# Output projection and first feed-forward product of a hybrid decoder layer: other banks, weight sums one tile ahead, token sums in another buffer, and column groups interleaved

## The chip, the cores and the metric

The kernel runs on one core of one Trainium2 chip. The metric is device time in microseconds (us) of the whole program. The engines are called PE (matrix products and transposes), DVE (vector), ACT (scalar functions and copies), POOL (GpSimd) and SP, which here only starts transfers between the chip's memory and the core's on-chip memory. Each engine takes its own instructions in order; an instruction whose input or output is not ready holds everything behind it on that engine.

## The reference

One decoder layer over 2048 tokens of width 1024, in float32:

```
nx = rmsnorm(x);  proj = nx @ w_in
o_a = gated linear attention heads;  o_b = dilated sliding-window attention heads
h = x + concat(o_a, o_b) @ w_out
nm = rmsnorm(h)
a = square(relu(nm @ w_ff1))        # 1024 -> 4096
h = h + a @ w_ff2                   # 4096 -> 1024
out = rmsnorm(h)
```

The change touches the third line (the output projection), the norm behind it, and the product with `w_ff1`, called FF1 below.

## The kernel before

Each float32 operand is split into a high part that the matrix engine takes and a low remainder: `split` (L483 to L485) writes the high part on ACT (L484) and the remainder on DVE (L485). `mm3` (L138 to L142) forms one product by three matmuls, high by high (L140), low by high (L141) and high by low (L142). A 128x512 split is thus one ACT and one DVE instruction.

Blocks of a matrix product are multiplied by a scheme of 7 products in place of 8: sums and differences of the four blocks of each operand are formed first, and the 7 products are added into accumulators that the blocks of the result share. The products are numbered 1 to 7 and are taken in the order 1, 2, 6, 5, 7, 3, 4.

The program runs in stages: the input projection (to about 520 us), attention and linear attention (to about 870), the output projection (to about 1067), FF1 for the first 1024 tokens (to about 1385) and for the second 1024 (to about 1690), then the second feed-forward product. The Python code writes the work in a certain order; a scheduler then places the instructions of each engine, so that the order on an engine is not always the order of the code. Accumulators lie in eight banks with tags: two "a", three "c", two "d", one "o". `ps("a")` takes the next bank with tag "a", and waits until its last reader is done.

The output projection starts with four rows of 128 tokens, the loop `for at in range(4)` from L1520, each as a plain product with 96 matmuls. `plain_rows` (L1512) transposes the mixed heads of a row with PE and splits them into `mT`, in two halves q = 0, 1 (banks "c" and "d"). Each row uses two accumulators with tag "a", to which a copy of `x` is added on DVE (L1541, tile `xh`). Beside it, `mix_wo` (from L1111) loads two chunks of `w_out` into `wtraw`, forms four differences on POOL (L1118), and splits them into `wb`; it is called once for each of the four rows, in that row. The first rows overlap with the end of the attention, whose branches are combined by L927 to L950 on DVE and POOL (tiles `gla`, `small`, `O`, `cmb`). The rest of the projection goes by 7 products: `product0(g)` for g from 14 to 55, of 12 matmuls each, with `prep0` forming the operand (`mcomb`) from raw copies that ACT makes of the transposed heads (`raw_block`, tile `ar`, L1467).

After each row `norm_row` (L1257) normalizes it, transposes it with PE (L1266), and lets ACT copy it into `bb` (L1267), which is stored to `hTD`. After each pair of rows `norm_sums` (L1270) forms four sums of the blocks on DVE in place in `bb` (L1274 to L1277) and stores them to `hTD` too. So FF1 later reads each of the 7 operand sums of the tokens from `hTD`: `token_pieces` (L1282) loads 14 pieces, two for each product, into `rb` (L1290), and splits each into `hb`, at a pace of 5 pieces in 4 jobs, counted from the argument `first`.

FF1 is a list of jobs: 32 groups of columns (16 for each token half) by 7 products, 12 matmuls a job. `prep1(at + 2)` forms the weights of the job two ahead: it splits a block of `w1raw` into one of four buffers `w1comb`, and at products 2 and 6 updates `w1raw` (L1366 to L1370). At products 7 and 4 it starts the load of the weights two groups on (L1351), one half of the group each; there are two such buffers, for even and odd groups. `product1` multiplies; accumulators come from `bank()`, which walks through the tags "a c d c a d c o", and their results leave by ACT (L1434) or DVE (L1436, L1440, L1444), then a relu and a square on ACT (L1425, L1426, L1449). Sums of the results for the next product are formed by `act_sums` (L1398), three steps a job.

Of the kernel before, what the change touches and what calls it, by code (L numbers as in the profile page):

```python
# [66 lines left out]
SUMS = [line.split() for line in SUMS.splitlines()]  # L67
EARLY = 5
SINGLE = {0: "a10", 1: "a13", 2: "a32", 22: "a01"}
# [45 lines left out]
def emit(tc, a, stop=99):  # L115
# [1135 lines left out]
    def store_T(t, *which):  # L1251
        half, i = t // HT, t % 4
        for j, q in which:
            SP.dma_start(hTD[half, j - 1][:, :, i * 128:i * 128 + 128], hb4[q])

# [13 lines left out]

    def norm_sums(t):  # L1270

        b11, b21, b12, b22 = hb4
        V.tensor_tensor(b12, b12, b11, op=OP.subtract)
        V.tensor_tensor(b22, b22, b12, op=OP.subtract)  # L1274
        V.tensor_tensor(b21, b21, b22, op=OP.subtract)
        V.tensor_tensor(b11, b22, b11, op=OP.subtract)
        store_T(t, (5, 2), (6, 3), (4, 1), (7, 0))  # L1277

    turns = [0]

    def token_pieces(half, first):

        parts_at = {}
        for n in range(14):
            parts_at.setdefault(first + 1 + n * 4 // 5, []).append(n)
        piece = lambda n: rb[n // 2 % 2][:, 1024 * (n % 2):1024 * (n % 2) + 1024]
# [5 lines left out]
        def step(at):  # L1292
            if at == first - 3:
                while len(rb) < 2:
                    rb.append(slot("rb"))
                for n in range(4):
                    load(n)
            for n in parts_at.get(at, ()):
                j = order[n // 2]
                if j not in TF:  # L1300
                    TF[j] = [slot(f"hb{j}", FR) for _ in range(2)]
                    TB[j] = [view(v, (4, 512)) for v in TF[j]]
                cs = slice(1024 * (n % 2), 1024 * (n % 2) + 1024)
                split(*[v[:, cs] for v in TF[j]], piece(n))
                load(n + 4)
# [35 lines left out]
    order = (1, 2, 6, 5, 7, 3, 4)  # L1341
    jobs1 = [(g, j) for g in range(2 * NP) for j in order]
    raw1, combs1, acc1 = [], [], []
# [59 lines left out]
    def product1(at):  # L1403
# [12 lines left out]
        if j in (1, 2, 5):  # L1416
            banks[j] = bank()
        p = banks[{6: 1, 7: 1, 4: 1, 3: 5}.get(j, j)]
        B, W = TB[j], combs1[at % 4]
# [23 lines left out]
        elif j == 3:  # L1443
            V.tensor_tensor(c12, p, X, op=OP.add)  # L1444
            square(c12)
            single(1)
        else:
            A.activation(c21, p, AF.Relu)
            A.activation(c21, c21, AF.Square)  # L1449
            single(2)  # L1450
            sums1.append(act_sums(half, q, both, SUMS[EARLY:] if par else SUMS[:EARLY]))

# [33 lines left out]
    def row_done(p, e):  # L1486
# [3 lines left out]
        if e:  # L1490
            norms.append((norm_sums, t))

# [19 lines left out]
    def plain_rows(p, e):  # L1512
        m = view(slot("mT", FR), (2, CH, 128))
        for q in range(2):
            split(*[m[:, i, 4 * q:4 * q + 4] for i in range(2)], mix_block(p, e, q, "cd"[q]))
        return m

    load_mix(0)
    nxt = plain_rows(0, 0)
    for at in range(4):  # L1520
        p, e = divmod(at, 2)
# [8 lines left out]
        if at == 1:  # L1530
            nxt = plain_rows(1, 0)
        mix_wo(at)
        b = [ps("a"), ps("a")]
        parts_ = 2 if at < 2 else 1
# [9 lines left out]
        if at == 3:  # L1544
            for q, e in ((0, 0), (1, 0), (0, 1), (1, 1)):
                raw_block(2, e, q)
            load_mix(3)
            for g in range(14, 17):
                prep0(g)
    half0, half1 = token_pieces(0, -7), token_pieces(1, 7 * (NP - 1))  # L1550
    for g in range(14, 56):
# [163 lines left out]
    for at in range(len(jobs1)):  # L1715
        prep1(at + 2)
        some_sums()
        product1(at)
# [100 lines left out]
```

## Time and profile before

| quantity | value |
|---|---|
| median of 3 runs | 2274.73 us (2273.97 to 2284.05) |
| profiled execution | 2281.68 us |
| its span, first to last instruction | 2279.8 us |
| PE busy | 2231.8 us (98%) |
| DVE busy | 1694.4 us (74%) |
| ACT busy | 1250.1 us (55%) |
| POOL busy | 502.2 us (22%) |
| mean granted clock of PE | 0.990 |

Times in the rows below are counted from the start of the span. In a timeline row the first number is the start, the second the length, then engine, line, operation, the tile written and the tiles read, the shape and a count; in brackets stands the idle time of the engine before it and what ended that idle time. A matmul row's length includes its tail in the array; matmuls that follow each other overlap, so their pace is read from the starts.

### The profile page before, as it was taken

What the parts mean: (1) busy time and instruction counts of PE and PEld (TensorE: products, weight loads), DVE (VectorE), ACT (ScalarE), POOL (GpSimd) and SP (SyncE); (2) the same over time, 40 slices, a digit from 0 to 9 for tenths busy, and PEclk for the clock granted to TensorE, in tenths of its full rate; (3) what the DMA queues carried; (4) which work ended last, traced back from release to release, by engine and by line L of the source; (5) the groups of instructions that cost most, each with busy time, mean ns of one, the idle gap of its engine ahead of it and who ended that gap; (6) DMA issues with size and microseconds to landing.
All of it is one profiled execution on the core that took longest, in us unless ns stands there. A gap on an engine that the chain in (4) does not pass through costs nothing.

```text
span 2279.8 us, 35292 instructions
## 1 busy us (share of the span) xinstructions
PE 2231.8 (98%) x12436; PEld 1928.3 (85%) x12436; DVE 1694.4 (74%) x3172; ACT 1250.1 (55%) x2483; POOL 502.2 (22%) x471
## 2 busy tenths in 40 slices
PE   9999999999999998899999999999999999999998
PEld 8978998799999997787788887888888888888876
DVE  8788877766777677767767678767786697566778
ACT  6665436425877873455555557555555433333435
POOL 1210002024385674200000000000006322032462
PEclk9999999999999999999999999999999999999999
DMA  6467754776757965677745456554479997767775
GB/s 206 129 186 243 250 156 133 221 239 221 225 194 237 285 204 196 216 228 249 225 128 164 128 164 210 157 176 146 144 250 278 315 303 266 220 236 254 255 260 177
DMA packets 363602, 482.80 MB, mean 212 GB/s; under 512 B 20197, under 2 KB 269558, under 8 KB 353184
## 3 DMA queue, kind: packets, MB, share of 16 engines
q1 hardware_dynamic: 358926, 471.89, 63.8%
q0 software_dynamic: 4352, 8.39, 2.0%
q8 instruction: 98, 1.61, 0.3%
q14 instruction: 80, 0.66, 0.1%
q10 hardware_dynamic: 146, 0.27, 0.0%
HBM read 330.74 MB, written 154.44 MB: 213 GB/s over the span
## 4 chain that ended last, share of the span: by engine, by line
PE 85%; DMA 5%; DVE 4%; issue 3%; ACT 2%; POOL 1%; SPq 0%; POOLq 0%; DVEq 0%; ACTq 0%
PE ps_a L141 8%; PE ps_a L140 8%; PE ps_a L142 8%; PE ps_c L141 8%; PE ps_c L142 8%; PE ps_c L140 8%; PE ps_a L890 4%; PE ps_d L141 4%; PE ps_d L140 4%; PE ps_d L142 4%; PE ps_o L142 4%; PE ps_o L141 4%; PE ps_o L140 4%; PE ps_d L871 3%; PE ps_c L853 2%
## 5 line engine op out<-in xcount | busy, mean ns | idle before, releaser
L1640 POOL TENSOR_TENSOR bs<-bs,rb 128x1024 f32<-128x1024 f32 x60 | 178.3, 2982 | 1036.9 <-DMA actD<-ring 792.5
L485 DVE TENSOR_TENSOR cb<-bs,cb 128x1024 fp32r<-128x1024 f32 x104 | 162.5, 1563 | 137.3 <-ACT cb L484 137.2
L484 ACT ACTIVATE cb<-bs 128x1024 fp32r<-128x1024 f32 x104 | 110.3, 1060 | 281.2 <-issue 141.0
L485 DVE TENSOR_TENSOR w1comb<-w1raw,w1comb 128x512 fp32r<-128x512 f32 x224 | 153.5, 687 | 87.7 <-ACT w1comb L484 87.7
L862 ACT ACTIVATE pe<-pe,O 128x256 f32<-128x256 f32 (+1 forms) x384 | 157.9, 453 | 53.8 <-DVE O L861 51.8
L890 PE MATMUL ps_a<-v,pt 128*128 128x65 f32 x1200 | 181.1, 255 | 5.4 <-ACT pt L878 5.4
L484 ACT ACTIVATE w1comb<-w1raw 128x512 fp32r<-128x512 f32 x224 | 139.5, 625 | 79.9 <-PE ps_c L142 28.9
L890 PEld LDWEIGHTS ps_a<-v,pt 128*128 128x128 f32 x1200 | 176.3, 196 | 7.2 <-ACT pt L878 6.0
L871 PE MATMUL ps_d<-ident,pe 128*128 128x128 f32 x600 | 160.8, 282 | 0.0
L861 DVE CUSTOM_DVE_ANT_0 pe<-ps_c,nb 128x256 f32<-128x256 f32 (+1 forms) x384 | 126.5, 360 | 44.2 <-PE ps_d L871 17.5
L284 ACT ACTIVATE wcomb<-wraw 128x512 fp32r<-128x512 f32 (+2 forms) x119 | 90.0, 757 | 99.3 <-PE ps_a L141 35.3
L140 PE MATMUL ps_c<-hb,w1comb 128*128 128x512 f32 x336 | 130.9, 390 | 0.0
L141 PE MATMUL ps_c<-hb,w1comb 128*128 128x512 f32 x336 | 130.7, 389 | 0.0
L142 PE MATMUL ps_c<-hb,w1comb 128*128 128x512 f32 x336 | 130.7, 389 | 0.0
L485 DVE TENSOR_TENSOR ca<-ra,ca 128x1024 fp32r<-128x1024 f32 x84 | 118.6, 1412 | 5.8 <-ACT ca L484 5.8
L141 PE MATMUL ps_c<-cb,ca 128*128 128x512 f32 x312 | 121.9, 391 | 0.0
L140 PE MATMUL ps_c<-cb,ca 128*128 128x512 f32 x312 | 121.9, 391 | 0.0
L142 PE MATMUL ps_c<-cb,ca 128*128 128x512 f32 x312 | 121.9, 391 | 0.0
L1425 ACT ACTIVATE acc<-acc 128x512 f32<-128x512 f32 x96 | 60.7, 632 | 93.6 <-DVE acc L1440 41.8
L871 PEld LDWEIGHTS ps_d<-ident,pe 128*128 128x128 f32 x600 | 110.4, 188 | 0.3
L349 POOL TENSOR_TENSOR acc<-acc,misc 128x264 f32<-128x264 f32 (+1 forms) x32 | 39.1, 1236 | 313.7 <-DVE acc L348 287.3
L142 PE MATMUL ps_a<-wcomb,tb 128*128 128x256 f32 (+1 forms) x344 | 97.7, 284 | 0.0
(457 smaller groups left out, 7195.8 us busy)
## 6 DMA issues: line engine op xcount, KB each, us to landing
ra<-actD SPq DMA_DIRECT2D x52, 1024.0 KB, 7.6
actD<-ring SPq DMA_DIRECT2D x176, 256.0 KB, 3.4
rb<-w_ff SPq DMA_DIRECT2D x88, 512.0 KB, 5.9
bs<-w_ff SPq DMA_DIRECT2D x72, 512.0 KB, 6.0
w1raw<-w_ff SPq DMA_DIRECT2D x64, 512.0 KB, 4.2
k<-kD SPq DMA_DIRECT2D x16, 1024.0 KB, 7.7
hTD<-bb SPq DMA_DIRECT2D x56, 256.0 KB, 3.9
rb<-hTD SPq DMA_DIRECT2D x28, 512.0 KB, 5.7
```

What stands on the lines that cost most here:

```text
L140: T.matmul(out, sh, mh, start=first, stop=False, **kw)
L141: T.matmul(out, sl, mh, start=False, stop=False, **kw)
L142: T.matmul(out, sh, ml, start=False, stop=last, **kw)
L284: A.activation(hi, src, AF.Copy, scale=sc)
L484: A.activation(hi, src, AF.Copy)
L485: V.tensor_tensor(lo, src, hi.bitcast(F32), op=OP.subtract)
L861: V.tensor_tensor_reduce(p, s, bias, scale=1.0, scalar=BIG, op0=OP.add, op1=OP.min, accum_out=nm)
L862: A.activation(p, p, AF.Exp, bias=nm, scale=-1.0)
L871: T.transpose(pb[:, i * 128:i * 128 + 128], src, ident)
L890: T.matmul(self.b.opsum[:, n % 4], self.pt[:, i * 128:i * 128 + 128], self.b.v[:, blk, cols], start=first, stop=last)
L1425: A.activation(v, v, AF.Relu)
L1640: (engines or ((G,), (V, V))[len(sums) - 1])[e].tensor_tensor(v, v, r, op=OP.add if op == "+" else OP.subtract)
```

## The change

It has five parts. (1) The transposes of the four plain rows all go through banks "c", and their accumulators alternate between "a" (even rows) and "d" (odd rows). (2) `mix_wo` is called one row earlier, for the first row ahead of the loop; in the last row the raw blocks, the load of the next mixed heads and the first two operands are formed ahead of that row's matmuls, not behind them. (3) `norm_sums` writes three of its four sums into the row's `xh` tile, which is no longer needed for the row itself, so they need not wait until the stores of `bb` have read it. (4) The pieces of the token operands come at a pace given by an argument: 110 hundredths of a job each in the first half, 130 in the second, with other starts. (5) In the first pair of groups, in the last of the first token half and in the first of the second half, the jobs of the two groups are interleaved, which also makes the banks belong to a group each, and the sums of the odd group come in two parts.

```diff
-EARLY = 5
+EARLY, LATE = 5, 12
...
-    def norm_sums(t):
+    def norm_sums(t, x):
         b11, b21, b12, b22 = hb4
+        t2, t4, t3 = [view(v, (4, 128)) for v in (x[:, 0, :512], x[:, 0, 512:], x[:, 1, :512])]
         V.tensor_tensor(b12, b12, b11, op=OP.subtract)
-        V.tensor_tensor(b22, b22, b12, op=OP.subtract)
-        V.tensor_tensor(b21, b21, b22, op=OP.subtract)
-        V.tensor_tensor(b11, b22, b11, op=OP.subtract)
-        store_T(t, (5, 2), (6, 3), (4, 1), (7, 0))
+        V.tensor_tensor(t2, b22, b12, op=OP.subtract)
+        V.tensor_tensor(t4, b21, t2, op=OP.subtract)
+        V.tensor_tensor(t3, t2, b11, op=OP.subtract)
+        store_T(t, (5, b12), (6, t2), (4, t4), (7, t3))
...
-    def token_pieces(half, first):
+    def token_pieces(half, first, pace):
         parts_at = {}
         for n in range(14):
-            parts_at.setdefault(first + 1 + n * 4 // 5, []).append(n)
+            parts_at.setdefault(first + n * pace // 100, []).append(n)
...
-            if at == first - 3:
+            if at == first - 4:
...
-    jobs1 = [(g, j) for g in range(2 * NP) for j in order]
+    apart = [(g, j) for g in range(2) for j in order]
+    mixed = [(0, 1), (0, 2), (0, 6), (1, 1), (0, 5), (1, 2), (0, 7), (1, 6), (0, 3), (1, 5), (0, 4), (1, 7), (1, 3), (1, 4)]
+    jobs1 = [(g + n, j) for g in range(0, 2 * NP, 2) for n, j in (mixed if g in (0, NP - 2, NP) else apart)]
...
-            banks[j] = bank()
-        p = banks[{6: 1, 7: 1, 4: 1, 3: 5}.get(j, j)]
+            banks[par, j] = bank()
+        p = banks[par, {6: 1, 7: 1, 4: 1, 3: 5}.get(j, j)]
...
+            if par:
+                sums1.append(act_sums(half, q, both, SUMS[EARLY:LATE]))
...
-            sums1.append(act_sums(half, q, both, SUMS[EARLY:] if par else SUMS[:EARLY]))
+            sums1.append(act_sums(half, q, both, SUMS[LATE:] if par else SUMS[:EARLY]))
...
     def plain_rows(p, e):
         m = view(slot("mT", FR), (2, CH, 128))
         for q in range(2):
-            split(*[m[:, i, 4 * q:4 * q + 4] for i in range(2)], mix_block(p, e, q, "cd"[q]))
+            split(*[m[:, i, 4 * q:4 * q + 4] for i in range(2)], mix_block(p, e, q, "c"))
...
     nxt = plain_rows(0, 0)
+    mix_wo(0)
     for at in range(4):
...
-        mix_wo(at)
-        b = [ps("a"), ps("a")]
+        if at < 3:
+            mix_wo(at + 1)
+        if at == 3:
+            for n in range(4):
+                raw_block(2, n % 2, n // 2)
+            load_mix(3)
+            for g in range(14, 16):
+                prep0(g)
+        b = [ps("ad"[e]), ps("ad"[e])]
...
         if at == 3:
-            for q, e in ((0, 0), (1, 0), (0, 1), (1, 1)):
-                raw_block(2, e, q)
-            load_mix(3)
-            for g in range(14, 17):
-                prep0(g)
-    half0, half1 = token_pieces(0, -7), token_pieces(1, 7 * (NP - 1))
+            prep0(16)
+    half0, half1 = token_pieces(0, -6, 110), token_pieces(1, 7 * (NP - 2) + 3, 130)
...
-        some_sums()
+        some_sums(4 if jobs1[at][0] // 2 in (NP // 2 - 1, NP // 2) and at % 14 < 5 else 3)
```

What the change moves in the finished program is seen best on the engines. First PE, at the end of row (0,0) of the projection and the start of row (0,1), before (a name such as `wo` or `wb` is a part of the weights, `mT` the transposed row):

```order
L140 MATMUL ps_a<-wo,mT 128x512
L141 MATMUL ps_a<-wo,mT 128x512
L142 MATMUL ps_a<-wo,mT 128x512
L140 MATMUL ps_a<-wb_9282,mT 128x512 [waits DVE_49]
L141 MATMUL ps_a<-wb_9282,mT 128x512
```

And at the same place after the change:

```order
L1337 MATMUL ps_c<-ident,O_9446 128x128 [waits DVE_49]
L141 MATMUL ps_a<-wo,mT 128x512
L142 MATMUL ps_a<-wo,mT 128x512
L140 MATMUL ps_a<-wo,mT 128x512
L141 MATMUL ps_a<-wo,mT 128x512
L142 MATMUL ps_a<-wo,mT 128x512
L141 MATMUL ps_d<-wb_9282,mT 128x512 [waits DVE_49]
L142 MATMUL ps_d<-wb_9282,mT 128x512
```

The new row writes to a bank "d" and waits for the row's own operand on DVE, no longer for the add that frees a bank "a"; one transpose of the attention's output (`O`) now stands inside the old row.

Second POOL, at the last combine of the attention (L927 to L950) and the first weight sums (L1118), before:

```order
L930 TENSOR_TENSOR gla<-gla,O_9446 128x8
L930 TENSOR_TENSOR gla<-gla,cmb 128x8 x2
L934 TENSOR_TENSOR gla<-gla,O_9446 128x8
L936 TENSOR_TENSOR gla<-gla,cmb 128x8
L937 TENSOR_TENSOR gla<-gla 128x8
L936 TENSOR_TENSOR gla<-gla,cmb 128x8
L937 TENSOR_TENSOR gla<-gla 128x8
L942 TENSOR_TENSOR gla<-gla 128x8 x3
```

And after:

```order
L1118 TENSOR_TENSOR wtraw<-wtraw 128x512
L930 TENSOR_TENSOR gla<-gla,O_9446 128x8
L930 TENSOR_TENSOR gla<-gla,cmb 128x8 x2
L1118 TENSOR_TENSOR wtraw<-wtraw 128x512
L934 TENSOR_TENSOR gla<-gla,O_9446 128x8
L936 TENSOR_TENSOR gla<-gla,cmb 128x8
L1118 TENSOR_TENSOR wtraw<-wtraw 128x512 x2
L937 TENSOR_TENSOR gla<-gla 128x8
L936 TENSOR_TENSOR gla<-gla,cmb 128x8
L937 TENSOR_TENSOR gla<-gla 128x8
L942 TENSOR_TENSOR gla<-gla 128x8 x3
```

The four sums of the first set stand between POOL's combine steps, where before the first of them came after the whole combine.

Third PE, at the end of the projection, where FF1's first jobs begin (`w1comb` their weights, `hb` the tokens, `xh` the last rows to be transposed), before:

```order
L140 MATMUL ps_d<-hb_11518,w1comb 128x512 [waits Activation_49]
L1266 MATMUL ps_c<-ident,xh 128x128 [waits DVE_49,PE_49]
L1266 MATMUL ps_c<-ident,xh 128x128 x3
L1266 MATMUL ps_c<-ident,xh 128x128 [waits PE_49]
L1266 MATMUL ps_c<-ident,xh 128x128 x3
L140 MATMUL ps_c<-hb_11451,w1comb 128x512 [waits PE_49]
L141 MATMUL ps_a<-hb_11428,w1comb 128x512 [waits DVE_49]
L142 MATMUL ps_a<-hb_11429,w1comb 128x512
```

And after:

```order
L1266 MATMUL ps_c<-ident,xh 128x128 [waits DVE_49,PE_49]
L1266 MATMUL ps_c<-ident,xh 128x128 x3
L1266 MATMUL ps_c<-ident,xh 128x128 [waits PE_49]
L1266 MATMUL ps_c<-ident,xh 128x128 x3
L140 MATMUL ps_c<-hb_11467,w1comb 128x512 [waits PE_49,Activation_49]
L140 MATMUL ps_d<-hb_11428,w1comb 128x512 [waits Activation_49]
L141 MATMUL ps_a<-hb_11428,w1comb 128x512 [waits DVE_49]
L142 MATMUL ps_a<-hb_11429,w1comb 128x512
```

In both, first matmuls of later jobs are moved ahead of the rest of the first job (bank "a"). The one into bank "d" is now that of the second group's first product, the fourth job, and it reads the first product's tokens.

More of the change, by code (lines that the diff above doesn't have):

```diff
@@ L1253, in store_T @@
         for j, q in which:
-            SP.dma_start(hTD[half, j - 1][:, :, i * 128:i * 128 + 128], hb4[q])
+            SP.dma_start(hTD[half, j - 1][:, :, i * 128:i * 128 + 128], hb4[q] if isinstance(q, int) else q)
     def norm_row(h, t):
```

2 lines of the change are left out of this document (1 added, 1 removed).

## The prediction

> **What bounds the kernel now.** I read the page's totals first, then the list of what the matrix engine (PE) waited for, then the granted clock in the stretches behind its long waits, and last the instructions of the engines it waited for.
>
> ```profile
> span 2279.8 us, 35292 instructions
> ...
> PE 2231.8 (98%) x12436; PEld 1928.3 (85%) x12436; DVE 1694.4 (74%) x3172; ACT 1250.1 (55%) x2483; POOL 502.2 (22%) x471
> ```
>
> PE is busy for 98% of the span, and the change leaves its matmuls as they are. So the change can win only what PE idles, and what it loses in clock, in the stretches that the diff touches: the first four rows of the output projection, the start of FF1, and the start of FF1's second token half. The waits of PE there are these (line, what it waited for, us in total, times, longest), the first row from 860 to 895 us, then two from 920 to 940, five from 1050 to 1100, four from 1376 to 1410:
>
> ```profile
> PE ps_a L140 <- DVE xh L1541: 4.0, 1, 4.0
> ...
> PE ps_c L1266 <- ACT ar L1467: 4.0, 1, 4.0
> PE ps_c L1336 <- ACT ar L1467: 2.2, 1, 2.2
> ...
> PE ps_a L140 <- ACT xs L1434: 5.4, 1, 5.4
> PE ps_d L141 <- DVE mcomb L485: 1.7, 1, 1.7
> PE ps_a L140 <- ACT w1comb L484: 1.5, 1, 1.5
> PE ps_d L140 <- ACT stats L173: 1.3, 1, 1.3
> PE ps_d L140 <- ACT acc L1434: 0.2, 1, 0.2
> ...
> PE ps_d L141 <- DVE w1comb L485: 1.7, 1, 1.7
> PE ps_o L140 <- ACT acc L1434: 0.9, 1, 0.9
> PE ps_d L140 <- ACT xs L1434: 0.5, 1, 0.5
> PE ps_d L140 <- ACT acc L1434: 0.5, 1, 0.5
> ```
>
> They sum to 4.0, 6.2, 10.1 and 3.6 us: 23.9 us. Behind the three longest the clock was low (stretch, its length, busy time of PE, PEld, DVE, ACT, POOL with counts, granted clock, DMA share, GB/s):
>
> ```profile
> 885.00:891.00 6.00, 5.96 (x15) 4.71 (x16) 5.99 (x10) 1.65 (x4) 0.00 (x0) 0.54 0.49 122
> 932.00:935.00 3.00, 3.00 (x9) 2.50 (x10) 2.50 (x4) 3.00 (x7) 0.00 (x0) 0.51 0.93 287
> 1091.00:1096.00 5.00, 4.79 (x12) 3.43 (x13) 1.77 (x3) 3.74 (x9) 0.00 (x0) 0.56 0.66 201
> ...
> 1060.00:1080.00 20.00, 17.17 (x79) 13.69 (x78) 18.07 (x24) 13.77 (x24) 0.00 (x0) 1.00 0.88 294
> 1080.00:1092.00 12.00, 6.44 (x30) 4.74 (x30) 11.99 (x15) 6.96 (x11) 0.00 (x0) 0.86 0.78 230
> 1110.00:1360.00 250.00, 250.00 (x1105) 207.08 (x1104) 182.49 (x371) 138.12 (x238) 0.00 (x0) 1.00 0.48 150
> ```
>
> A clock of 0.54 over 6 us loses 0.46 x 6 = 2.8 us; the next two rows lose 1.5 and 2.2: 6.5 us. In 1060 to 1080, where PE waited 1.3 and 1.5 us, the clock stayed at 1.00, so a wait that shrinks to that size costs its own length only. The ceiling of the change is 23.9 + 6.5 = 30.4 us, 1.3% of the time. The last row shows FF1 in its steady state: PE full, DVE at 0.73.
>
> The Trainium skill gives the clock a rule ("TensorE: Matmul & The Clock Gate", Part 1: The HAM clock gate): after an idle window of about 3.4 us the array runs at half rate until it has been busy for about 3.4 us. By that figure a slow stretch costs an estimated 1.7 us and the ceiling would be 29.0; the rows say 30.4, and the 4.0 us and 5.4 us waits that were followed by 0.54 and 0.56 agree with the threshold.
>
> **The change, place by place.**
>
> *First rows of the projection.* PE's row (0,1) reused row (0,0)'s banks and so waited for the add of xh, which stood on DVE behind the last combine of the attention:
>
> ```profile
> 880.44 0.39 PE L141 MATMUL ps_a<-wo,mT 128*128 128x512 f32 x1
> 880.67 0.39 PE L142 MATMUL ps_a<-wo,mT 128*128 128x512 f32 x1
> 885.04 0.80 PE L140 MATMUL ps_a<-wb,mT 128*128 128x512 f32 x1 [3.98 <-DVE xh L1541]
> ...
> 879.41 0.17 DVE L937 TENSOR_TENSOR gla<-gla 128x8 f32<-128x8 f32 x1
> 879.61 1.16 DVE L936 TENSOR_TENSOR gla<-gla,cmb 128x8 f32<-128x8 f32 x1
> ...
> 884.31 0.68 DVE L1541 TENSOR_TENSOR xh<-ps_a,xh 128x512 f32<-128x512 f32 x1
> 884.91 0.68 DVE L485 TENSOR_TENSOR mT<-ps_d,mT 128x512 fp32r<-128x512 f32 x1
> 885.51 0.68 DVE L950 TENSOR_TENSOR O<-O,cmb 128x512 f32<-128x512 f32 x1
> ...
> 878.05 3.92 POOL L1118 TENSOR_TENSOR wtraw<-wtraw 128x512 f32<-128x512 f32 x3
> ...
> 1052.89 1.03 PE L1266 MATMUL ps_c<-ident,xh 128*128 128x128 f32 x8
> ```
>
> With banks "d" the row starts at 880.9 without the add. Its first half is 24 matmuls, paced 0.23 us (880.44 to 880.67): 5.5 us, and 8 transposes among them, 0.8 us by the last row (eight in 1.03 with the tail of the last): PE reaches the second half at 887.2. That half needs the low part of mT's second half, on DVE. It began at 884.91 and was done at 885.6. Now four weight splits stand ahead of the combine (0.6 us apart each, as 884.31, 884.91 and 885.51 show: 2.4 us) and one L950 too (0.6): done at 888.6, a wait of 1.4 us in place of 4.0 + 2.8. Unknown is what POOL does to that chain, since four weight sums now run between POOL's own combine steps. The same 128x8 operation took 1.16 us and 0.17 us in neighbouring rows, the long one while POOL worked, but POOL worked through most of the chain before as well. The wait has 0 as lower end (the chain is faster) and 4 with a slow clock as upper end; I take 2.0, nearer to the sum of rows. Gain 6.8 - 2.0 = 4.8, between 0 and 6.8.
>
> A rule of the Trainium skill speaks against this step ("SBUF — State Buffer", Who interferes with whom): DVE and GpSimd share a port pair as an exclusive lock for a whole instruction, and a DVE operation with two SBUF inputs contends for it. By it each of the four moved sums blocks the chain for its full length; what that gives is the first rival below.
>
> *Weight sums one tile ahead.* The two waits at 926.8 and 932.0 come from ACT: its copies of the raw blocks (L1467) stand behind splits that wait for POOL's sums.
>
> ```profile
> 913.99 6.06 POOL L1118 TENSOR_TENSOR wtraw<-wtraw 128x512 f32<-128x512 f32 x4 [14.32 <-DMA wtraw<-w_out]
> 920.62 6.68 POOL L1118 TENSOR_TENSOR wtraw<-wtraw 128x512 f32<-128x512 f32 x4 [0.58 <-DMA wtraw<-w_out]
> ...
> 925.66 0.63 ACT L484 ACTIVATE wb<-wtraw 128x512 fp32r<-128x512 f32 x1 [1.04 <-POOL wtraw L1118]
> ...
> wtraw<-w_out SPq DMA_DIRECT2D x8, 512.0 KB, 6.8
> ```
>
> Each set is now summed one row of the projection earlier: 48 matmuls x 0.23 = 11 us, more than the 6.2 us lost. What stays is the last set: its load waits for a slot that PE frees, and 14.3 us of POOL's wait for the load in the first row says such a load can set the pace. A load of 6.8 us (its median in the page) and sums of 6.1 us need 12.9 us against the 11: 2 us late, at most. I leave 2.0. The raw copies of the next tiles now come ahead of that row's matmuls, so ACT has room. Gain 6.2 + 1.5 - 2.0 = 5.7, between 3 and 7.7.
>
> *Start of FF1.* DVE is full from 1080 to 1092 (11.99 of 12 us), and ACT, which must free the bank that PE wants, stands behind a piece's load:
>
> ```profile
> 1089.16 1.06 ACT L484 ACTIVATE hb<-rb 128x1024 fp32r<-128x1024 f32 x1 [2.41 <-DMA rb<-hTD]
> ...
> 1082.01 1.21 DVE L485 TENSOR_TENSOR hb<-rb,hb 128x1024 fp32r<-128x1024 f32 x1
> ...
> DVE bb L1274 <- DMA hTD<-bb: 2.8, 1, 2.8
> ...
> w1raw<-w_ff SPq DMA_DIRECT2D x64, 512.0 KB, 4.2
> ```
>
> A piece costs DVE 1.2 us. A job is 12 matmuls, 2.73 us, of which steady work takes 0.73. With a piece each 0.8 jobs (2.18 us) the pieces add 0.55, and DVE is asked for 1.28 of its time; at 1.10 jobs they add 0.40. Interleaving two groups asks for each new piece half as often, so the 14 pieces need not be there by the seventh job. Token sums that no longer overwrite what is being stored take away the 2.8 us wait in the third row; DVE idled there for nothing. I count no gain for it alone, since it feeds the same chain. All this is the same amount of DVE work in a longer stretch: still close to full, so I leave two waits of the size of 1.3 and 1.5.
>
> The added wait: the second group's weights are needed at the fourth job, not the eighth, and PE's first matmul of that job stands ahead of the rest of the first job. The load follows a slot whose last reader is the product before the last of the projection. PE needs 2.7 us for the last product, 0.8 for eight transposes and 0.4 for two matmuls, 3.9 us after that reader's product ends; the data need 4.2 us and a 0.6 us split after the reader itself, up to 2.7 us earlier. So PE waits 0 to 0.9 us, more if the load is slower than its median (5.8 us were it to take 9). I take 1.3. Gain 10.1 + 2.2 - 2.8 - 1.3 = 8.2, between 4 and 12.3.
>
> *Start of the second half.* Fourteen pieces, one each 0.8 jobs, give a backlog of 0.28 x 11 jobs x 2.73 = 8.4 us, of which 3.6 showed as waits, so nearly 5 us are hidden by lead. At 1.30 jobs (3.55 us) pieces add 0.34, DVE is asked for 1.07 over 18 jobs, and the backlog is 3.4 us: within the lead. I leave 1.0 for the output sums that four instead of three steps bring forward. Gain 2.6, between 0 and 3.6.
>
> *At nothing:* the other order of the raw blocks, and norm rows held in xh longer; DMA queues have the time that the loads ahead leave. If xh's later release makes its next load late, a projection row waits.
>
> Sum: 4.8 + 5.7 + 8.2 + 2.6 = 21.3 us. The profiled execution took 2281.7 us (its span of 2279.8 and 1.9 around it), 7.0 above the median of the three runs (2274.7). 2281.7 - 21.3 - 7.0 = 2253.4.
>
> **The rivals.**
>
> *POOL's sums block the combine.* Each of four sums (1.3 us each by 3.92 over 3) holds DVE: the second half of mT comes 5.2 us later, PE waits 1.4 + 5.2 = 6.6 us and loses 2.8 of clock. The place then costs 9.4, where it cost 6.8: 7.4 worse than forecast, 2260.8. For it: 1.16 against 0.17 us. Against: POOL was there before as well.
>
> *The second group's weights come late.* 5.8 us of wait and 2.2 of clock instead of 1.3: 6.7 worse, 2260.1. For it: a load behind others on one queue; against: the median of 4.2 us.
>
> *The pace changes nothing.* DVE is asked for the same work, and the waits of FF1 only move: neither 8.2 nor 2.6 is won, 2264.2. For it: DVE's 11.99 of 12; against: nearly all of FF1 behind 1110 has 27% of DVE free.
>
> *Slower: weight reloads of the interleaved groups are late.* Raw weights were reloaded eight jobs before use; five reloads (around the first pair, and the pairs where the token half changes) now have four: 10.9 us. The load takes 4.2, the split 1.3 (0.63 on ACT and 0.68 on DVE by the rows above), so 5.4 us may pass in the queue of SP, which waits in order:
>
> ```profile
> 1385.28 7.99 SPq L1290 DMA_DIRECT2D rb<-hTD  x4
> SPq L1400 <- DVE ring L1398: 14.6, 8, 9.7
> ```
>
> A hold of 9.7 us makes a reload 4.3 us late and costs 2.5 of clock: 6.8 each. It decides from a hold of 5.4 us, and four late reloads eat the gain; all five cost 34 us, 12.7 more than is won: 2287. Against: the mean hold in the second row is 1.8 us, and pieces are fewer per job.
>
> **How the numbers follow.** Forecast as summed 0.52, alone between 2245 and 2266; POOL blocking 0.15; late second weights 0.14; pace without effect 0.10; reloads late 0.09. About 0.5% (11.4 us) can be told from no change here: faster is below 2263.4, slower above 2286.1. The first case lies below for 0.48 of its 0.52, the next two for 0.17 of 0.29, the fourth for 0.02: faster 0.67. Slower are the last case's five late reloads and mishaps of two kinds together, 0.09; the rest, 0.24, is no change. The range begins at the ceiling, 2274.7 - 30.4 = 2244, and ends at 2275, the fourth case with the projection's 10.5 lost as well, that is no gain at all; above it lies 0.12.
>
> **What would show it.** Right: no wait at the start of row (0,1), one of about 2 us in the middle of it, with the clock at 1.00 behind it; no wait of PE for ar L1467; no wait above 2 us from 1060 to 1100; DVE below 0.95 around the half's change. Wrong: a wait above 3.4 us for mT with DVE's 128x8 operations above 1 us; a wait of PE for w1comb at the fourth job; waits for w1comb behind w1raw's load at jobs 14, 98 and 112; new waits between 940 and 1050 from xh's loads.

## The result, and the profile after

The changed kernel took 2267.9 us (median of 8 runs, 2263.9 to 2270.3), the kernel before 2281.85 us in the runs beside it (median of 8, 2274.0 to 2284.1). The ratio is 0.9944, 95% interval 0.9929 to 0.9960: faster by 0.56%, some 13 us. The forecast was faster, with a gain of 21.3 us and a time of 2253.4. The profiled execution of the changed kernel took 2265.1 us, with a span of 2263.3.

The page's totals and PE's waits over the whole span after the change (columns as before: us in total, times, longest):

```profile
span 2263.3 us, 35306 instructions
...
PE 2226.8 (98%) x12436; PEld 1924.6 (85%) x12436; DVE 1696.3 (75%) x3172; ACT 1249.3 (55%) x2483; POOL 503.4 (22%) x471
...
PE ps_d L141 <- DVE mT L485: 3.3, 1, 3.3
...
PE ps_c L1266 <- DVE xh L1261: 2.0, 2, 1.5
PE ps_c L1337 <- ACT ar L1472: 1.7, 1, 1.7
PE ps_c L140 <- DVE acc L1443: 1.4, 1, 1.4
...
PE ps_o L140 <- ACT w1comb L484: 1.2, 1, 1.2
PE ps_c L140 <- ACT xs L1437: 0.9, 1, 0.9
PE ps_a L140 <- ACT acc L1437: 0.9, 1, 0.9
...
PE ps_d L140 <- ACT w1comb L484: 0.8, 2, 0.5
```

The wait for xh at row (0,1) is gone, and so are the one of 5.4 us at FF1's start and all of those near 1380 to 1404. A wait of 3.3 us for mT has come in the first rows, and nine small ones (1.5 us at most) between 1073 and 1132.

Waits alone don't tell what a place costs. A wait is listed from the end of the last matmul's 0.39 us, while the next could have started 0.23 us after it; the second matmul behind a wait starts 0.11 us late; and the clock can fall. So I took for each place its length, less the pace of the matmuls that were started in it at full clock (0.227 us for 128x512, 0.107 for a 128x128 transpose). I call this the loss; it is good to about half a microsecond. To compare executions, the first two places are counted from the same matmul of the attention, and FF1's start from FF1's first matmul:

| place | loss before | loss after | gain | gain as predicted |
|---|---|---|---|---|
| first rows (50 us from the last attention products) | 6.4 | 5.4 | 1.0 | 4.8 |
| next 22 us (raw copies) | 8.1 | 2.6 | 5.5 | 5.7 |
| from there to FF1's start | 3.2 | 1.9 | 1.3 | none |
| FF1's start, from 8 us ahead of its first matmul, 92 us | 11.6 | 10.9 | 0.7 | 8.2 (with the row above) |
| change of the token half | 5.0 | 0.0 | 5.0 | 2.6 |
| second feed-forward product, not touched | 7.1 | 5.5 | 1.6 | none |

These make 15.1 of the 16.5 us that lie between the two spans. By the medians the change is worth 13 to 14, since executions of one kernel differ by several us also where its code is the same.

The window of the lost clock in the first rows, and one around the change of the half (stretch, length, busy of PE, PEld, DVE, ACT, POOL, clock, DMA share, GB/s):

```profile
890.00:897.00 7.00, 6.73 (x23) 5.40 (x24) 5.76 (x10) 4.59 (x10) 1.15 (x1) 0.76 0.77 250
...
1360.00:1430.00 70.00, 70.00 (x310) 57.96 (x310) 61.82 (x117) 48.01 (x79) 0.00 (x0) 1.00 0.66 216
```

PE is full through the second stretch. Two places gave much less than forecast: the first rows and FF1's start. The experiments go to them.

### The profile page after: what moved, and what is told of

It reads as the page before. It is cut to its first block, busy times and chain, and to the rows that moved or that the text cites. A ratio compares the mean times of both kernels' runs of the same rounds, so it can differ in the third digit from the quotient of the medians.

```text
span 2263.3 us, 35306 instructions
## 1 busy us (share of the span) xinstructions
PE 2226.8 (98%) x12436; PEld 1924.6 (85%) x12436; DVE 1696.3 (75%) x3172; ACT 1249.3 (55%) x2483; POOL 503.4 (22%) x471
## 4 chain that ended last, share of the span: by engine, by line
PE 86%; DVE 5%; DMA 4%; issue 3%; POOL 1%; ACT 1%; POOLq 0%; SPq 0%; DVEq 0%; ACTq 0%
PE ps_a L141 8%; PE ps_a L142 8%; PE ps_a L140 8%; PE ps_c L140 7%; PE ps_c L142 7%; PE ps_c L141 7%; PE ps_d L141 4%; PE ps_d L142 4%; PE ps_d L140 4%; PE ps_a L890 4%; PE ps_o L142 4%; PE ps_o L140 4%; PE ps_o L141 4%; PE ps_d L871 3%; PE ps_c L853 2%
## 5 line engine op out<-in xcount | busy, mean ns | idle before, releaser
L140 PE MATMUL ps_c<-hb,w1comb 128*128 128x512 f32 x320 | 124.7, 390 | 2.3 <-DVE acc L1443 1.4
L142 PE MATMUL ps_c<-hb,w1comb 128*128 128x512 f32 x320 | 124.5, 389 | 0.0
L141 PE MATMUL ps_c<-hb,w1comb 128*128 128x512 f32 x320 | 124.5, 389 | 0.0
```

The lines of the kernel that those rows point to most:

```text
L140: T.matmul(out, sh, mh, start=first, stop=False, **kw)
L141: T.matmul(out, sl, mh, start=False, stop=False, **kw)
L142: T.matmul(out, sh, ml, start=False, stop=last, **kw)
```

## The experiments

All of them are edits of the changed kernel. Runs of one group lay beside runs of the kernel before, and "ratio" is against these; the changed kernel's own is 0.9944.

### The first rows: who makes mT late?

In the changed kernel, the last combine on DVE, the operand behind it, and what POOL and PE did meanwhile, from its timeline:

```profile
885.57 3.45 DVE L948 TENSOR_TENSOR cmb<-cmb,gla 128x512 f32<-128x512 f32 x2
888.94 0.68 DVE L950 TENSOR_TENSOR O<-O,cmb 128x512 f32<-128x512 f32 x1
889.54 0.68 DVE L485 TENSOR_TENSOR mT<-ps_c,mT 128x512 fp32r<-128x512 f32 x1
...
882.19 6.28 POOL L1118 TENSOR_TENSOR wtraw<-wtraw 128x512 f32<-128x512 f32 x4
...
890.27 0.69 PE L141 MATMUL ps_d<-wo,mT 128*128 128x512 f32 x1 [3.30 <-DVE mT L485]
```

The two steps of L948 took 3.45 us, where the same two took 1.29 at 883.10 in the kernel before. Beside them run four weight sums, and they are not the first set, which the prediction spoke of, but the second: its load also moved up one row.

**Without the second set's sums** (the loads and splits stay, the four subtractions are left out):

```diff
-            G.tensor_tensor(dst, x, y, op=OP.subtract)
+            if c != 1:
+                G.tensor_tensor(dst, x, y, op=OP.subtract)
```

> The changed kernel without the four weight sums of the second set (chunks 1 and 5 of w_out): they are loaded and split, but not subtracted, so the output differs there. Theory (those sums on POOL hold DVE's last combine): L948's two steps take about 1.3 us in place of 3.45, PE's wait for mT falls from 3.3 us to about 1.1 and the clock behind it stays at 1.00; the time is 3 to 4 us shorter than the changed kernel's. Rival (DVE is late because four splits and one more L950 stand ahead of that operand): the two steps take 1.3 us, but PE's wait stays above 2.5 us, or the steps keep their 3.45 us; time within 1.5 us.

Measured: 2263.5 us, ratio 0.9913 (0.9892 to 0.9934). The steps of L948, then the operand:

```profile
881.54 1.29 DVE L948 TENSOR_TENSOR cmb<-cmb,gla 128x512 f32<-128x512 f32 x2
882.75 0.69 DVE L950 TENSOR_TENSOR O<-O,cmb 128x512 f32<-128x512 f32 x1
883.35 0.68 DVE L485 TENSOR_TENSOR mT<-ps_c,mT 128x512 fp32r<-128x512 f32 x1
```

PE's 3.3 us wait is gone, and the first rows lose 1.8 us in place of 5.4. For the mechanism the theory held. The time says less than its 7 us (by the ratios) suggest: the next place loses some 2 us more than in the changed kernel (4.7 against 2.6), and of the 7.7 us between the two spans 2.6 lie ahead of the last attention products and 2.3 in the second feed-forward product, which the edit does not touch.

L948 is not the only step that these sums can hold. In four of the kernels below, whose first rows are the code of the changed kernel (norm beside the row, first pair apart, token sums in place, change of the half as before), the second set ran beside the 128x8 steps and ended before L948. From the first of them:

```profile
886.32 5.30 POOL L1118 TENSOR_TENSOR wtraw<-wtraw 128x512 f32<-128x512 f32 x4
...
889.30 2.34 DVE L942 TENSOR_TENSOR gla<-gla 128x8 f32<-128x8 f32 x3
...
892.16 1.28 DVE L948 TENSOR_TENSOR cmb<-cmb,gla 128x512 f32<-128x512 f32 x2
```

The three L942 steps took 2.34 us, where they took 0.32 without the second set's sums. L948 took 1.28 in all four, and PE still waited 3.6 us for mT. So the wait hangs on the second set running beside the combine, whichever steps it meets.

**The second set held back.** To keep the sums, their load is made to wait, by a write of ACT into the buffer that needs mT's second half:

```diff
         raw = slot("wtraw")
+        if c == 1:
+            A.activation(raw[:, D - 4:D + 4], nxt[:, 0, CH - 1, :8].bitcast(F32), AF.Copy)
         SP.dma_start(raw[:, :D], wo[:, c])
```

> The changed kernel with the load of the second set of weights held back: ACT first writes eight numbers of mT's second half for row (0,1) into the buffer, so the load starts at about 880.5 in place of 871.5 and POOL's second set of sums after the last combine on DVE has ended. Theory (the collision with POOL makes that combine late, the sums themselves have time to spare): L948's two steps take about 1.3 us, PE's wait for mT falls from 3.3 us to about 1, the clock behind it stays at 1.00, no longer wait for the raw copies; about 4 us shorter than the changed kernel. Rival (the chain of loads and sums has no time to spare): the wait for the raw copies near 926 grows by 2 us or more, and the time is the same within 1.5 us.

Measured: 2266.8 us, ratio 0.9941 (0.9926 to 0.9956). DVE and POOL, and PE's waits from 866 to 940:

```profile
884.54 1.28 DVE L948 TENSOR_TENSOR cmb<-cmb,gla 128x512 f32<-128x512 f32 x2
...
886.30 1.30 POOL L1120 TENSOR_TENSOR wtraw<-wtraw 128x512 f32<-128x512 f32 x1 [3.59 <-DMA wtraw<-w_out]
...
PE ps_c L1339 <- ACT ar L1474: 2.4, 1, 2.4
PE ps_a L141 <- DVE mT L485: 1.3, 1, 1.3
PE ps_a L140 <- ACT mcomb L484: 0.3, 1, 0.3
```

The mechanism is as the theory has it: the steps take 1.28 us, the wait at row (0,1) is gone (the 1.3 is earlier, at 872.6), and the first rows lose 1.9. But the next place loses 3.5 in place of 2.6, and FF1's start 12.7 in place of 10.9, because the clock was 0.76 over the 7 us behind its last wait (from 1128.5) where it was 1.00 in the changed kernel. Of the 3.5 us little is left, and the time is the rival's.

**The operand formed on POOL.** The same wait, attacked from the other side:

```diff
+            hi, lo = [m[:, i, 4 * q:4 * q + 4] for i in range(2)]
+            src = mix_block(p, e, q, "c")
+            A.activation(hi, src, AF.Copy)
+            if (p, e, q) == (0, 1, 1):
+                raw = view(scr[:, :512], (4, 128))
+                A.activation(raw, src, AF.Copy)
+                G.tensor_tensor(lo, raw, hi.bitcast(F32), op=OP.subtract)
+            else:
+                V.tensor_tensor(lo, src, hi.bitcast(F32), op=OP.subtract)
```

> The changed kernel with one split taken off DVE: the remainder of the second half of mT for row (0,1) is formed on POOL, from a copy that ACT makes in the free half of gs, and it stands there ahead of the second set of weight sums. Theory (that one operand behind the combine on DVE is all that row (0,1) waits for): POOL has it at about 883.5, PE's 3.3 us wait and the low clock behind it go, nothing takes their place before 917; the time is about 5 us shorter than the changed kernel's. Rival (DVE's lateness shows elsewhere, at the adds of xh that free the banks of row (1,0)): PE waits for xh L1554 at about 893 instead, 2 us or more, and the time is within 2 us.

Measured: 2269.1 us, ratio 0.9934 (0.9917 to 0.9952). PE's waits from 866 to 940:

```profile
PE ps_c L1337 <- ACT ar L1472: 2.1, 1, 2.1
PE ps_a L140 <- ACT mT L1522: 1.1, 1, 1.1
PE ps_c L1337 <- ACT bb L1267: 1.1, 1, 1.1
PE ps_c L1266 <- DVE xh L1261: 0.6, 1, 0.6
PE ps_c L1337 <- DMA mx<-mixD: 0.5, 1, 0.5
PE ps_a L141 <- DVE mT L1528: 0.2, 1, 0.2
```

The 3.3 us wait went, and five smaller ones came in the rows behind it, because DVE was still late with everything else (its two L948 steps took 1.78 us each). The loss there is 5.1 against 5.4. The rival held, with other waits than it named.

**Every set in its own row, as before:**

```diff
-    mix_wo(0)
     for at in range(4):
...
-        if at < 3:
-            mix_wo(at + 1)
+        mix_wo(at)
```

> The changed kernel with each set of weight sums formed in its own row as before (the raw blocks stay ahead of the last row's matmuls). Theory (the second set of sums, now running beside DVE's last combine, is what made that combine late): the two L948 steps of that combine take about 1.3 us together in place of 3.45, PE's wait for mT in row (0,1) falls from 3.3 us to below 1; the waits for ACT's raw copies come back, about 6 us with a low clock behind them; sum about 1 to 3 us longer than the changed kernel. Rival (the sums one row ahead are what gained nothing, the raw blocks ahead of the row did): the waits for raw copies stay below 2 us, and the time is about 4 us shorter than the changed kernel's.

Measured: 2277.2 us (10 runs), ratio 0.9971 (0.9957 to 0.9985), so some 6 us slower than the changed kernel, more than the theory's 1 to 3. The L948 steps took 0.68 us each and the wait for mT went, as the theory had it. Instead the next norm stood on DVE behind a weight split that waited, by way of ACT, for POOL, and PE behind that:

```profile
895.82 1.20 DVE L485 TENSOR_TENSOR wb<-wtraw,wb 128x512 fp32r<-128x512 f32 x1 [4.36 <-ACT wb L484]
896.94 2.28 DVE L1261 SCALAR_TENSOR_TENSOR xh<-xh,stats,gs 128x1024 f32<-128x1024 f32 x1
...
899.37 1.94 PE L1266 MATMUL ps_c<-ident,xh 128*128 128x128 f32 x8 [4.86 <-DVE xh L1261]
```

The next place lost 8.0 us, as before the change (8.1). So the sums one row ahead are what won the 5.5 us there; the raw blocks ahead of the row alone won nothing.

**The banks of before:**

```diff
-            split(*[m[:, i, 4 * q:4 * q + 4] for i in range(2)], mix_block(p, e, q, "c"))
+            split(*[m[:, i, 4 * q:4 * q + 4] for i in range(2)], mix_block(p, e, q, "cd"[q]))
...
-        b = [ps("ad"[e]), ps("ad"[e])]
+        b = [ps("a"), ps("a")]
```

> The changed kernel with the banks of before: transposes of the plain rows in "c" and "d", accumulators of all rows in "a"; everything else stays. Theory (the second half of row (0,1) waits for DVE behind the last combine, whatever bank it uses, and in the changed kernel that combine ends some 5 us later than before): PE waits for xh L1554 at the start of the row from about 881 until about 890.8, 9 to 10 us in place of 3.3, with a low clock behind it, and the time is about 6 us longer than the changed kernel's. Rival (the banks are worth nothing because the row waits for mT either way): PE's wait stays within 1 us of 3.3, the time within 1 us.

Measured: 2270.1 us, ratio 0.9948 (0.9932 to 0.9964). The theory failed and the rival comes nearer: the row waits for mT either way, here 1.9 us at 891.9, behind one of 2.6 us at 875.0 in the row ahead, and the time can't be told from the changed kernel's. PE's waits from 866 to 940, and the add that frees the bank, with the first step of the combine that stands behind it now:

```profile
PE ps_a L141 <- DVE mT L485: 4.4, 2, 2.6
PE ps_c L1337 <- ACT ar L1472: 0.8, 1, 0.8
...
880.11 0.69 DVE L1554 TENSOR_TENSOR xh<-ps_a,xh 128x512 f32<-128x512 f32 x1 [1.17 <-PE ps_a L142]
880.72 0.22 DVE L930 TENSOR_TENSOR gla<-gla,O 128x8 f32<-128x8 f32 x1
```

The scheduler now places the add ahead of the combine, so a row in bank "a" no longer waits for it, and it waits for mT like the row in bank "d". The banks save about 2 us of loss in the first rows, and in the time too little to be told.

### FF1's start: why so little?

In the changed kernel, SP's transfers, DVE's two long waits, and the times of the transfers to landing, from 1070 to 1086 us (hD) and from 1084 to 1106 (w1raw):

```profile
1076.51 0.84 SPq L1493 DMA_DIRECT2D hD<-xh  x1
...
1086.78 2.59 SPq L1291 DMA_DIRECT2D rb<-hTD  x3
...
1091.39 1.39 SPq L1354 DMA_DIRECT2D w1raw<-w_ff  x1
...
1083.73 1.28 DVE L1261 SCALAR_TENSOR_TENSOR xh<-xh,stats,gs 128x1024 f32<-128x1024 f32 x1 [4.66 <-DMA hD<-xh]
1084.94 0.68 DVE L485 TENSOR_TENSOR w1comb<-w1raw,w1comb 128x512 fp32r<-128x512 f32 x1
1085.54 4.62 DVE L485 TENSOR_TENSOR hb<-rb,hb 128x1024 fp32r<-128x1024 f32 x4
...
1102.93 0.69 DVE L1369 TENSOR_TENSOR w1raw<-w1raw 128x512 f32<-128x512 f32 x1 [6.56 <-DMA w1raw<-w_ff]
...
hD<-xh SPq DMA_DIRECT2D x1, 512.0 KB, 7.1
w1raw<-w_ff SPq DMA_DIRECT2D x3, 512.0 KB, 6.8
```

The same instruction in the kernel before:

```profile
1077.27 1.29 DVE L1261 SCALAR_TENSOR_TENSOR xh<-xh,stats,gs 128x1024 f32<-128x1024 f32 x1 [1.18 <-DMA hD<-xh]
```

L1261 normalizes the last row in place, so it waits until the row's store has read it, 7.1 us after its issue. DVE stands for 4.7 us, with the splits of four token pieces behind. Their buffers are free late, SP starts the next three loads at 1086.8, and the weight reload comes behind them. DVE then stands for 6.6 us more, and afterwards has more to do than PE leaves it time for.

**The norm written beside the row:**

```diff
-        V.scalar_tensor_tensor(h, h, r, gM, op0=OP.mult, op1=OP.mult)
+        V.scalar_tensor_tensor(scr, h, r, gM, op0=OP.mult, op1=OP.mult)
...
-                T.transpose(pv[:, c], h[:, (4 * q + c) * 128:(4 * q + c + 1) * 128], ident)
+                T.transpose(pv[:, c], scr[:, (4 * q + c) * 128:(4 * q + c + 1) * 128], ident)
```

> The changed kernel, but a row's norm (L1261) is written into the free half of gs, not over the row itself, so DVE need not wait until the row's store to hD has read it. Theory (that wait, 4.7 us of DVE at 1083.7 in the changed kernel, holds the splits of four token pieces, these hold the next loads on SP, and the weight reload behind them comes late, for which DVE idles 6.6 us at 1102.9): DVE's waits for hD and for w1raw of that size go, PE's waits of 1.5 at 1085 and 1.5 at 1103 go, those of 0.9, 0.9 and 1.4 from 1116 to 1131 shrink to below 1.5 together; about 5 us shorter than the changed kernel. Rival (the reload is late because the interleaved pair asks for it four jobs after its start, whatever DVE does): DVE still idles over 5 us for w1raw near 1103, PE's waits from 1103 to 1131 stay within 1 us of their 5.0, and 1 to 2 us are won.

Measured: 2260.0 us (2257.7 to 2263.1), ratio 0.9908 (0.9888 to 0.9928). The norm no longer waits, and the wait for the reload is short; PE's waits from 1066 to 1138 are three:

```profile
1080.24 1.28 DVE L1261 SCALAR_TENSOR_TENSOR gs<-xh,stats,gs 128x1024 f32<-128x1024 f32 x1
...
1100.13 0.69 DVE L1369 TENSOR_TENSOR w1raw<-w1raw 128x512 f32<-128x512 f32 x1 [1.48 <-DMA w1raw<-w_ff]
...
PE ps_c L140 <- DVE acc L1443: 1.5, 1, 1.5
PE ps_a L140 <- ACT w1comb L484: 1.0, 1, 1.0
PE ps_d L140 <- ACT w1comb L484: 0.3, 1, 0.3
```

From the raw copies to the end of FF1's start it lost 6.9 us in place of 12.8, and the time fell by 0.36% of the kernel before, about 8 us, more than the 5 expected. The theory held, but for the last small waits: those of 0.3 and 1.5 us near 1125 stayed, and the 1.8 together are above its 1.5. This kernel is faster than the changed one.

**The first pair of groups one after the other**, with its pieces 0.8 jobs apart (the slower pace is only possible with the interleaving, since the seventh job needs the last piece):

```diff
-    jobs1 = [(g + n, j) for g in range(0, 2 * NP, 2) for n, j in (mixed if g in (0, NP - 2, NP) else apart)]
+    jobs1 = [(g + n, j) for g in range(0, 2 * NP, 2) for n, j in (mixed if g in (NP - 2, NP) else apart)]
...
-    half0, half1 = token_pieces(0, -6, 110), token_pieces(1, 7 * (NP - 2) + 3, 130)
+    half0, half1 = token_pieces(0, -6, 80), token_pieces(1, 7 * (NP - 2) + 3, 130)
```

> The changed kernel with the first pair of FF1's groups one after the other and its token pieces 0.8 jobs apart, as before; the two pairs around the change of the token half stay interleaved. Theory (interleaving the first pair only exchanged PE's waits for others: it costs the late reload and what follows it, about 7 us, and saves about 10): no waits after 1100, 7 to 10 us lost from 1050 to 1100, the time within 3 us of the changed kernel's. Rival (the interleaving is what won at FF1's start, and the other parts did not): the 13.7 us that the kernel before lost there come back in full, 2.6 us longer than the changed kernel.

Measured: 2266.1 us, ratio 0.9939 (0.9923 to 0.9954): no different. PE's waits from 1066 to 1138 are now 1.2, 0.7, 0.7 and 0.6 us, all ahead of 1101. The loss is 6.2 us to 46 us behind the start of this place and 1.0 after it, against 4.0 and 6.9 with the interleaving. So interleaving the first pair moved the loss to later, and in this place it even lost more; the time can't tell the two kernels apart, as the theory had it.

**The token sums in place, as before** (the three destinations of `norm_sums` are blocks of `bb` again):

> The changed kernel with the token sums in place in bb, as before. Theory (these waits of DVE for the stores are on no path that PE waits for): DVE waits again for hTD stores, 2 to 3 us at a time, PE's waits change by less than 1 us and the time by less than 1.5 us. Rival (they fed the FF1 start): PE loses 2 to 4 us more from 1060 to 1135, the time is as much longer.

Measured: 2273.3 us (10 runs), ratio 0.9967 (0.9953 to 0.9980), 5 us slower than the changed kernel: the rival held, and this part is worth more than the prediction gave it, which was nothing by itself. About half of the loss comes ahead of FF1, at the raw copies (5.1 us in place of 2.6), where DVE waited 2.6 us for such a store. DVE's waits for those stores, and the next in the list, from 1045 to 1137 us:

```profile
DVE bb L1275 <- DMA hTD<-bb: 6.5, 2, 5.0
DVE xh L1261 <- DMA hD<-xh: 3.7, 1, 3.7
```

PE waited 2.1 us for the first weights, 1.9 for a norm and 2.4 for the reload.

### The change of the token half

**As before**, with the groups apart, pieces 0.8 jobs apart and three steps of sums a job:

```diff
-    jobs1 = [(g + n, j) for g in range(0, 2 * NP, 2) for n, j in (mixed if g in (0, NP - 2, NP) else apart)]
+    jobs1 = [(g + n, j) for g in range(0, 2 * NP, 2) for n, j in (mixed if g in (0,) else apart)]
...
-    half0, half1 = token_pieces(0, -6, 110), token_pieces(1, 7 * (NP - 2) + 3, 130)
+    half0, half1 = token_pieces(0, -6, 110), token_pieces(1, 7 * (NP - 1) + 1, 80)
...
-        some_sums(4 if jobs1[at][0] // 2 in (NP // 2 - 1, NP // 2) and at % 14 < 5 else 3)
+        some_sums()
```

> The changed kernel with the start of the second token half as before: groups one after the other in the two pairs around it, pieces 0.8 jobs apart, three steps of sums per job. Theory (this part won all of what PE lost there, 3.6 us of waits and about 1.4 us of restarts): waits of about 3.6 us return between 1365 and 1400, the time is 4 to 5 us longer than the changed kernel's. Rival (the waits there went because FF1's first half ran at another phase): no waits return, the time is the same within 1 us.

Measured: 2272.9 us (10 runs), ratio 0.9969 (0.9959 to 0.9979), 5.7 us by the ratios. The waits from 1360 to 1430 are back (1.0, 0.9, 0.8, 0.5, 0.2, 0.2) and the loss there is 5.3 us, as in the kernel before. The theory held: this part is a gain of 5 us, the slow pace, the interleaving and the fourth step of sums together; which of the three did it was not separated.

### Together

Three kernels put the findings together.

> The norm written beside the row, as in the run before, and also the first pair of FF1's groups one after the other with pieces 0.8 jobs apart. Theory (with the hD wait gone the reload is in time, and the interleaving costs or saves little): 5 to 7 us lost from 1050 to 1138, as with the norm alone (6.4), the time within 1.5 us of 2260. Rival (the losses of the interleaving and of the hD wait are separate and add): 1 to 3 us lost there, and 3 to 5 us shorter than with the norm alone.

> The norm written beside the row and the second set of weights held back, the first pair interleaved as in the changed kernel. Theory (two separate losses, one at the first rows, one at FF1's start): both gains add, 4 us and 8 us: about 2256. Rival (they share a path): no more than 1 us below 2260.

> All three: norm beside the row, second set of weights held back, first pair one group after the other. Theory: the first rows as with the weights held back alone, FF1's start as with the norm and the first pair undone; with the theories of those runs about 2256, with their rivals between 2252 and 2260.

| kernel | median, us | ratio (95%) | loss: first rows, next 22 us, to FF1, FF1's start in two parts |
|---|---|---|---|
| norm beside the row | 2260.0 | 0.9908 (0.9888 to 0.9928) | 4.8, 1.4, 0.5, 2.4, 4.0 |
| with the first pair apart | 2261.2 | 0.9917 (0.9902 to 0.9932) | 5.1, 0.5, 0.7, 6.2, 0.0 |
| with the second set held back | 2258.8 | 0.9906 (0.9891 to 0.9921) | 1.6, 2.9, 0.6, 3.1, 3.8 |
| all three | 2257.2 | 0.9902 (0.9886 to 0.9919) | 1.8, 2.9, 0.8, 5.9, 1.0 |

The fastest is all three at once, about 1% below the kernel before; against the norm alone none of the three can be told apart. With the norm beside the row the first pair apart or interleaved makes no difference (first theory of the group). Holding the weights back wins 3.2 us in the first rows and gives 1.5 back at the raw copies; the rest is too small for the interval, so the rival of that run is nearer than its theory.

## Why the prediction was wrong

The direction and the ceiling held, the size did not: 21.3 us were forecast and 13 measured, about 0.6 of it.

- *The base.* The term "7.0 above the median of the three runs" failed. With five more runs of the kernel before, its median is 2281.85, right at the profiled execution. Two low ones of three were taken for the level. This made 7 of the 14.5 us between forecast and result.
- *First rows, 4.8, measured 1.0.* The row lost its wait for the add of xh, as predicted, and waited for mT, as predicted. The terms of the sum (four splits and one L950 ahead) gave 888.6 for that operand, and 890.2 was measured. The sum counted 0.6 us too many, since the L950 took the place of the add of xh; the missing 2.2 are L948's 3.45 in place of 1.29. The step that failed is "four weight sums now run between POOL's own combine steps": with those, L948 began only 2.5 us later than before, as four splits alone make 2.4, while the second set, which moved up as well and which the prediction did not set beside the combine, held the rest of it. Without its sums the first rows lost 1.8 us, a gain of 4.6, which is nearly the forecast. The rival of POOL had the right mechanism with the wrong set, and priced it at 6.6 us of wait; it was 3.3 to 3.6, and the low clock cost 1.7 (0.24 x 7) in place of 2.8. The clock behind the wait, which the prediction put at 1.00, was 0.76. The Trainium skill's rule on the shared port pair ("SBUF — State Buffer", Who interferes with whom) is borne out in this place: with the sums taken away or moved, the same two operations, which read two inputs from on-chip memory, fell from 3.45 to 1.29 and 1.28 us.
- *Raw copies, 5.7, measured 5.5.* Right, and by the mechanism named: with the sums back in their own row the loss was 8.0 again. The wait that stayed was 1.7, where 2.0 was left. (A row of the loop has 48 matmuls, as the prediction takes it, and not the 96 of the kernel's description: two accumulators, eight chunks, three matmuls each.)
- *FF1's start, 8.2, measured 2.0* (with the stretch ahead of it). The step "close to full, so I leave two waits of the size of 1.3 and 1.5" failed. DVE was not full: it idled 4.7 and 6.6 us. A norm that waits for a store to read its row was in the profile before (1.2 us for hD<-xh), and I had passed it over; it grew to 4.7, the store landing 7.1 us after its issue. With the norm written beside the row the two places lost 6.9 us in place of the 14.8 before the change, a gain of 7.9, nearly the forecast. The wait for the second group's weights, which the prediction set at 1.3, did not come at the first matmul into bank "d" (1058.9); the next for weights in such a bank, at 1074.0, was 0.5 us. The pieces' pace and the interleaving, on which the term rested, won nothing by themselves in the first half, as the rival of the pace had it for this place; the sums out of place, counted as nothing, are worth 5 us in the time.
- *Change of the half, 2.6, measured 5.0.* The waits went in full, as the mechanism named would have it; its parts were not tested apart. The size was short because a listed wait is not all that is lost: 3.6 us of waits were 5.0 of loss with the clock at 1.00. The step "a wait that shrinks to that size costs its own length only" failed here.
- *Slower by late reloads.* Its place was named, its cause was not: of the five reloads one held PE (1.2 us), by the chain behind the norm, and none at the change of the half.

The rest is spread: 1.6 us came in the second feed-forward product, which the change does not touch.

## What to carry to other kernels

When a producer's load is moved earlier, ask what its consumer on POOL will then run beside, step by step, and not only what the moved instruction itself stands beside. An operation in place on a tile that is still being stored puts a DMA's landing on the engine's own queue: write beside it, if there is room. A wait in the profile that is small today is a candidate for tomorrow's bound when the queue ahead of its transfer grows; list such waits for each engine that the path leans on, not only for PE.

## What the runs showed of the hardware

Two 128x512 operations of DVE with both inputs in on-chip memory took 1.29 us alone and 3.45 to 3.47 beside POOL's sums of the same size; POOL's four took 6.28, where they took 5.30 beside the 128x8 steps. Both sides lost. A 128x8 operation with both inputs there took 0.17 us alone and 1.14 to 1.25 beside such a sum. Adds of DVE that read one input from an accumulator bank kept their 0.68 us beside POOL's sums (the add of xh at 896.35 in the changed kernel, inside a sum of 1.74 us from 895.85).

After waits of 3.3 to 4.9 us PE's clock was 0.76 over the next 7 us in all seven executions looked at, a loss of 1.7 us, less than the 2.8 behind the 4.0 us wait before the change. It can also fall after shorter ones. At the end of FF1's start PE waits 0.3 us for weights and, within a microsecond, 1.4 to 1.8 us for an accumulator, in the same code. Behind that the clock was 0.76 in seven executions (that of the norm beside the row and six more) and 1.00 in three (that of the changed kernel and two more):

```profile
1126.00:1133.00 7.00, 5.78 (x18) 4.65 (x19) 3.84 (x6) 3.03 (x6) 0.00 (x0) 0.76 0.06 19
...
1131.00:1138.00 7.00, 6.78 (x30) 5.64 (x31) 4.96 (x10) 3.53 (x6) 0.00 (x0) 1.00 0.16 31
```

The first row is the norm beside the row, with 1.5 us of wait, the second the changed kernel, with 1.4; a wait of 1.8 us (without the second set's sums) left the clock at 1.00 too. So the prediction's statement that waits of that size leave the clock alone does not hold in general, and the length of the wait does not tell when it holds; what does is not shown. Nor do these rows bear out the threshold that the prediction cites.
